# A 16-expert layer: the weights of experts 6 to 15 loaded as 32 KB rows into five buffers in place of 16 KB rows into ten

## The chip, the core and the metric

The kernel runs on one core of a Trainium2 chip. The metric is the device time of one execution in microseconds (us). The core has four compute engines with a queue each (TensorE, here PE; VectorE, DVE; ScalarE, ACT; GpSimd, POOL), a queue that only issues transfers (SyncE, SP), and 16 DMA engines that move data between the main memory (HBM) and the on-chip memory (SBUF, 128 partitions).

## The reference, cut to what matters

One layer on 512 tokens of width 1024, all in float32: a mixer (attention, convolution, gated linear attention), then a mixture of 16 experts. Each expert picks its 64 tokens, and its three weight matrices are read once.

```
x    = layer_norm(alpha * x + merged @ w_out) * ln_mix_g + ln_mix_b
aff  = softmax(x @ router_w);  gate, idx = top_k(aff.T, 64)      # per expert
xs   = x[idx]                                                    # 16 x 64 x 1024
h    = silu(xs @ w_gate) * (xs @ w_up)                           # w_gate, w_up: 16 x 1024 x 2048
y    = (h @ w_down) * gate                                       # w_down: 16 x 2048 x 1024
out  = layer_norm(alpha * x + scatter_add(y, idx))
```

The three matrices of an expert have 8 MiB each; all experts together have 402.7 MB.

## The kernel before, in words

The mixer and the router take the first third of the time. Then the experts run one after the other, `e` from 0 to 15, and each in three passes, `kind` in "gud" (gate, up, down), of eight steps `k` each. A step multiplies with one 1 MiB slice of the weight: 8 KB in each of the 128 partitions. `ff_mm` (L1218, its matmul L1223) does a step of gate and up, `down` (L1226, its matmul L1232) one of down, and `last_down` (L1254, its matmul L1265) one of the last expert's down pass.

Weights arrive as "pairs" (L824): 2 MiB transfers, 16 KB contiguous in each partition, for two steps each; so a pass has four pairs and an expert twelve. `load_pairs` (L828) issues them on SP in the order of use, through `load` (L78, L79 in the profile). Each takes one of the ten 16 KB buffers of the pool `pairs` (L35, NPAIR at L17), and waits until PE has done the two steps that used that buffer. The ten are used in one fixed rotation, which is not their order in memory: counted by address, the compiled program takes the buffers 6, 2, 8, 1, 0, 4, 3, 7, 9, 5 again and again, and the ten pairs from the third gate pair of expert 5 to its last down pair lie in this order. The compiled program also gives every transfer one of eight completion counters in turn, and a transfer's issue waits until the transfer that had the same counter before has landed.

What a partition holds is set by `halves` (L820): partition p holds r consecutive rows of the weight, r = 2 for gate and up (two rows of 2048) and r = 4 for down (four rows of 1024). Since gate and up multiply with a slice whose partition p stands for row 256 c + 2 p + b, the gathered tokens must be put in the same order: `gather` (L1167, its matmul L1171) reads every second column of the tokens, and its ACT instruction scales by the matching columns of `pkt`. In the same way the hidden values are transposed for the down pass with a column step of 4 (L1414). Tokens are gathered for two experts at a time, one pair of experts ahead: those of experts 6 and 7 in expert 5.

The last expert (`LAST`, 15) differs: its down weight is loaded by column blocks (first 512 columns, then twice 256) in ten transfers of 1 MiB to 256 KB with 2 KB and 1 KB rows, so that the first columns can be finished while the last ones arrive. The work on an expert's output is put off: `combine` (L1208, matmuls L1213 and L1214) adds a pair of experts to the sum in the up pass of the next even expert, one token block before each of the steps 5, 6 and 7 and one behind, and in the gate pass of expert 15. `st_pair` makes the transposed selection that `combine` needs, at the beginning of these passes.

PE's order is the order of the program text. SP's queue holds nothing but transfers, in the order above.

Of the kernel before, what the change touches and what calls it, by code (L numbers as in the profile page):

```python
# [5 lines left out]
F32 = mybir.dt.float32  # L6
# [17 lines left out]
PK_BIAS, PK_NG, PK_CW, PK_SINK, PK_RW, PK_LN, PK_N = 0, 4, 8, 20, 28, 156, 188  # L24
PK_G1, PK_B1 = PK_LN, PK_LN + 8


@with_exitstack
def tile_hybrid_layer(ctx, tc, pk, w2p, xT, x, wlv, wa, wak, wmb, wout, eg, eu, ed, gb, out):
    nc = tc.nc  # L30
# [3 lines left out]
    cpool = ctx.enter_context(tc.tile_pool(name="consts", bufs=1))  # L34
    dpool = ctx.enter_context(tc.tile_pool(name="pairs", bufs=NPAIR))  # L35
    spool = ctx.enter_context(tc.tile_pool(name="slots", bufs=NSLOT))
# [32 lines left out]
    def P(name):  # L69
        return psum.tile([128, 512], F32, name=name, tag="ps")  # L70
# [714 lines left out]
    def xr_(tb):  # L785
        return xres[tb // 2][:, tb % 2, :]
# [37 lines left out]
    chunk = {}  # L824
    pairs = [(e, kind, j) for e in range(NE) for kind in "gud" for j in range(4) if e or kind != "d" or j < 2]
    npair = [0]

    def load_pairs(upto):  # L828
        for e, kind, j in pairs[npair[0]:upto]:
            t = chunk[e, kind, j] = D(f"e{e}{kind}{j}", [128, 4096])[0]  # L830
            if kind != "d" or e < NE - 1:
                load(t, halves(e, kind, j))
                continue

            n, c = (8, slice(0, 512)) if j < 2 else (16, slice(j * 256, (j + 1) * 256))
            t = chunk[e, kind, j] = t.rearrange("p (f d) -> p f d", f=n)
            src = ed[e].rearrange("(f p) d -> p f d", p=128)[:, j % 2 * 8 if j < 2 else 0:, c]
            cuts = (0, n // 2, n) if j < 3 else (0, 8, 12, 14, 16)
            for f0, f1 in zip(cuts, cuts[1:]):
                load(t[:, f0:f1], src[:, f0:f1])  # L840
        npair[0] = max(npair[0], upto)

# [5 lines left out]
    def part(e, kind, k):  # L848

        t = chunk[e, kind, k // 2]  # L850
        return t[k % 2] if isinstance(t, list) else t[:, k % 2 * 2048:k % 2 * 2048 + 2048]

    for u in range(24):
# [6 lines left out]
        if u == 23:  # L860
            wo_split(0, 0)
            wo_split(0, 1)
            load_wo(1, None)
            load_pairs(EARLY)
            load_x()
        if u == 0:
            accs = D("macc", Q, Q)
# [299 lines left out]
    def gather(i, d):  # L1167

        p = P("pxg")
        for tb in range(4):  # L1170
            PE.matmul(p[:, 0:128], xr_(tb)[:, every2(d)], Sg[:, tb].rearrange("p a b -> p (a b)"),  # L1171
                      start=tb == 0, stop=tb == 3)
        A.activation(XG[i % 2][:, d, :], p[:, 0:128], AF.Identity, scale=pkt[:, PK_G1 + d:PK_G1 + d + 1],  # L1173
                     bias=pkt[:, PK_B1 + d:PK_B1 + d + 1])

# [67 lines left out]

    LAST = NE - 1
    gb2 = xres[0]
# [8 lines left out]
    def last_down(k):  # L1254

        b = max(k // 2 - 1, 0)
        n, m = (4, 512) if b == 0 else (8, 256)
        f0 = k * 4 if b == 0 else k % 2 * 8
        w = chunk[LAST, "d", k // 2][:, k % 2 * n:k % 2 * n + n]
        if f0 == 0:  # L1260
            st["py"] = P("py")
        py = st["py"][:, 0:m]
        for i in range(n):
            f, g = f0 + i, i % 2
            PE.matmul(py[g * 64:(g + 1) * 64, :], hT[:, f % 8, f // 8 * 64:f // 8 * 64 + 64], w[:, i, :],  # L1265
                      start=f < 2, stop=f >= 14)
        if f0 == 0 and b:
            last_combine(b - 1)
        gl = gate[:, LAST:LAST + 1]
        if f0 + n == 16:  # L1270
            h, l = ylast(yh, b), ylast(yl, b)
# [58 lines left out]
    for e in range(NE):  # L1330
        for kind in "gud":
# [6 lines left out]
            for k in range(8):  # L1338
# [3 lines left out]
                elif e % 2 == 1 and e < LAST:  # L1342
# [6 lines left out]
                    if s == 23:  # L1349
                        gates(i)  # L1350
                if e == 0 and kind == "u" and k == 0:
                    load_pairs(len(pairs))
# [44 lines left out]
            elif kind == "u":  # L1397
# [12 lines left out]
                for t in range(0, 8, n):  # L1410
                    p = P("pht")
                    for i in range(n):
                        c0, step = (t * 128 + i, 4) if e < LAST else ((t + i) * 128, 1)
                        PE.transpose(p[:, i * 128:(i + 1) * 128], hb[:, c0:c0 + 127 * step + 1:step], ident)  # L1414
# [72 lines left out]
def host_arrays(x, w_in, attn_sink, conv_w, gla_gate_w2, gla_gate_b, gla_norm_g, w_branch_attn, w_branch_conv,  # L1487
# [23 lines left out]
    for b in ("g", "c", "a"):  # L1511
        for j in range(8):
# [8 lines left out]
    rw = f(router_w)[0].reshape(4, 128, 2, 16).transpose(1, 0, 2, 3).reshape(128, 128)  # L1521
    col = lambda a: f(a)[0].reshape(8, 128).T
    col2 = lambda a: f(a)[0].reshape(4, 128, 2).transpose(1, 0, 2).reshape(128, 8)
    pk = np.concatenate([bias, ng, cw, rows(f(attn_sink)[0]), rw, col2(ln_mix_g), col2(ln_mix_b),
# [7 lines left out]
             eg=f(expert_w_gate)[0], eu=f(expert_w_up)[0], ed=f(expert_w_down)[0],  # L1532
             gb=np.concatenate([f(ln_ffn_g), f(ln_ffn_b)], 0))
    return {k: np.ascontiguousarray(v) for k, v in a.items()}
# [17 lines left out]
```

## Time and profile before

| | us |
|---|---|
| median of 3 runs (1434.36 to 1434.84) | 1434.37 |
| the profiled execution, its own time | 1432.91 |
| its span, first to last instruction | 1431.1 |
| PE busy in the span | 1356.2 |

The profiled execution spends 1.8 us outside its span. The page cuts the span into 40 slices of 35.8 us; a 9 in the DMA row means that the 16 DMA engines were busy at least 90% of the slice. TensorE's granted clock is at its full level nearly throughout.

### The profile page before, as it was taken

The numbers are of one execution on the slowest core, as the hardware profiler recorded it, in microseconds if no ns is written. First come the engines' busy times: TensorE is split into PE (matmuls) and PEld (weight loads), VectorE is DVE, ScalarE is ACT, GpSimd is POOL, SyncE is SP. The second block draws the span as 40 slices with busy tenths as digits, with TensorE's granted clock in tenths as the row PEclk, the third lists the DMA queues.
The fourth block names the chain that finished last, engine by engine and source line by source line (L and its number), as shares of the span: only waits on it lengthen the run. The fifth ranks groups of instructions, "written<-read, shape, count | busy, mean of one in ns | idle before, by whom it ended". The sixth has DMA issues, their size and how long they took to land.

```text
span 1431.1 us, 17334 instructions
## 1 busy us (share of the span) xinstructions
PE 1356.2 (95%) x7429; PEld 764.9 (53%) x7429; DVE 416.8 (29%) x875; ACT 291.7 (20%) x554; POOL 30.1 (2%) x57
## 2 busy tenths in 40 slices
PE   9999999999999899999999999988989898898997
PEld 8777777888888753443453443333333342343333
DVE  5593975323445513112012012002011010100314
ACT  4744544222233210110110110110000110011011
POOL 0010000000000010000000000000000000000002
PEclk9999999999999999999999999999999999999999
DMA  6120122223239789999999999999999999999995
GB/s 232 46 89 31 64 76 69 88 94 104 89 125 403 297 333 404 429 428 426 430 426 429 427 428 427 427 427 429 427 428 427 429 428 427 429 427 428 426 413 193
DMA packets 45456, 449.32 MB, mean 314 GB/s; under 512 B 4314, under 2 KB 8538, under 8 KB 19524
## 3 DMA queue, kind: packets, MB, share of 16 engines
q1 hardware_dynamic: 44804, 447.01, 75.6%
q8 instruction: 58, 0.95, 0.3%
q10 hardware_dynamic: 576, 1.21, 0.2%
q14 instruction: 18, 0.15, 0.0%
HBM read 446.11 MB, written 2.10 MB: 313 GB/s over the span
## 4 chain that ended last, share of the span: by engine, by line
PE 57%; DMA 37%; DVE 3%; SPq 1%; ACT 1%; issue 0%; DVEq 0%; POOL 0%; ACTq 0%
PE pgt L1223 7%; PE py L1232 6%; PE pup L1223 6%; PE pa L274 3%; PE pm L874 3%; PE pm L876 3%; PE pm L875 3%; DMA e8d<-in_ed_dram 3%; DMA e12g<-in_eg_dram 3%; PE pa L276 3%; PE pa L275 3%; DMA e9u<-in_eu_dram 3%; DMA e13u<-in_eu_dram 3%; DMA e10d<-in_ed_dram 3%; DMA e14u<-in_eu_dram 3%; DMA e6d<-in_ed_dram 3%
## 5 line engine op out<-in xcount | busy, mean ns | idle before, releaser
L1216 DVE TENSOR_TENSOR acc<-acc,pcb 128x512 f32<-128x512 f32 x64 | 41.1, 683 | 216.9 <-PE pcb L1214 216.9
L1401 DVE TENSOR_TENSOR hbt<-pup,hbt 128x512 f32<-128x512 f32 (+1 forms) x34 | 22.3, 660 | 279.0 <-PE pup L1223 278.9
L1171 PEld LDWEIGHTS pxg<-Sg,xres 128*128 128x128 f32 x512 | 65.2, 196 | 51.5 <-issue 46.8
L274 PE MATMUL pa<-xh,wb 128*128 128x512 f32 x200 | 82.7, 414 | 0.0
L1171 PE MATMUL pxg<-Sg,xres 128*128 128x128 f32 x512 | 76.2, 292 | 6.5 <-DVE Sg L1154 6.5
L276 PE MATMUL pa<-xh,wb 128*128 128x512 f32 x200 | 78.3, 391 | 0.0
L275 PE MATMUL pa<-xl,wb 128*128 128x512 f32 x200 | 78.2, 391 | 0.0
L874 PE MATMUL pm<-xh,wm 128*128 128x512 f32 x192 | 74.8, 390 | 0.0
L875 PE MATMUL pm<-xl,wm 128*128 128x512 f32 x192 | 74.7, 389 | 0.0
L876 PE MATMUL pm<-xh,wm 128*128 128x512 f32 x192 | 74.7, 389 | 0.0
L1241 DVE SCALAR_TENSOR_TENSOR yl<-py,small,late 64x512 fp32r<-64x512 f32 x30 | 22.5, 750 | 140.9 <-ACT late L1240 140.9
L1240 ACT ACTIVATE late<-py,small 64x512 fp32r<-64x512 f32 x30 | 20.5, 682 | 194.4 <-PE py L1232 182.3
L1173 ACT ACTIVATE xgb<-pxg,pk 128x128 f32<-128x128 f32 x32 | 14.6, 458 | 155.8 <-PE pxg L1171 155.8
L1415 ACT COPY hbt<-pht 128x512 f32<-128x512 f32 (+1 forms) x18 | 9.8, 550 | 169.9 <-PE pht L1414 169.4
L1173 ACT ACTIVATE xga<-pxg,pk 128x128 f32<-128x128 f32 x32 | 14.6, 457 | 142.6 <-PE pxg L1171 142.6
L274 PEld LDWEIGHTS pa<-xh,wb 128*128 128x128 f32 x200 | 37.5, 188 | 11.2 <-issue 2.9
L234 DVE TENSOR_TENSOR wm<-wr,wm 128x1536 fp32r<-128x1536 f32 x24 | 42.1, 1752 | 4.1 <-ACT wm L231 4.1
L1388 ACT ACTIVATE hbt<-pgt 128x512 f32<-128x512 f32 x32 | 19.0, 597 | 117.1 <-PE pgt L1223 117.1
L276 PEld LDWEIGHTS pa<-xh,wb 128*128 128x128 f32 x200 | 37.6, 188 | 8.4
L275 PEld LDWEIGHTS pa<-xl,wb 128*128 128x128 f32 x200 | 37.6, 188 | 6.4
L874 PEld LDWEIGHTS pm<-xh,wm 128*128 128x128 f32 x192 | 36.0, 188 | 7.6 <-issue 0.2
L876 PEld LDWEIGHTS pm<-xh,wm 128*128 128x128 f32 x192 | 36.0, 188 | 7.6
(426 smaller groups left out, 2264.6 us busy)
## 6 DMA issues: line engine op xcount, KB each, us to landing
wr<-in_wmb_dram SPq DMA_DIRECT2D x24, 768.0 KB, 4.3
wr<-in_wa_dram SPq DMA_DIRECT2D x12, 1024.0 KB, 4.8
e0g<-in_eg_dram SPq DMA_DIRECT2D x4, 2048.0 KB, 14.8
e0u<-in_eu_dram SPq DMA_DIRECT2D x4, 2048.0 KB
e1g<-in_eg_dram SPq DMA_DIRECT2D x4, 2048.0 KB, 7.7
e1u<-in_eu_dram SPq DMA_DIRECT2D x4, 2048.0 KB, 15.6
e1d<-in_ed_dram SPq DMA_DIRECT2D x4, 2048.0 KB, 15.0
e2g<-in_eg_dram SPq DMA_DIRECT2D x4, 2048.0 KB, 12.1
```

The source lines that it names most:

```text
L234: sp2[u] = V.tensor_sub(l, raw2[u], f32(h))
L274: PE.matmul(p, w[:, 0, k, :], XH(k), start=k == 0, stop=False)
L275: PE.matmul(p, w[:, 0, k, :], XL(k), start=False, stop=False)
L276: PE.matmul(p, w[:, 1, k, :], XH(k), start=False, stop=k == 7)
L874: PE.matmul(p, h[:, k, :], XH(k), start=k == 0, stop=False)
L875: PE.matmul(p, h[:, k, :], XL(k), start=False, stop=False)
L876: PE.matmul(p, l[:, k, :], XH(k), start=False, stop=k == 7)
L1171: PE.matmul(p[:, 0:128], xr_(tb)[:, every2(d)], Sg[:, tb].rearrange("p a b -> p (a b)"), start=tb == 0, stop=tb == 3)
L1173: A.activation(XG[i % 2][:, d, :], p[:, 0:128], AF.Identity, scale=pkt[:, PK_G1 + d:PK_G1 + d + 1], bias=pkt[:, PK_B1 + d:PK_B1 + d + 1])
L1216: V.tensor_add(r, r, p)
L1223: PE.matmul(p[c][g * 64:(g + 1) * 64, :], l, w[:, g * 1024 + c * 512:g * 1024 + c * 512 + 512], start=k == 0, stop=k == 7)
L1232: PE.matmul(p[g * 64:(g + 1) * 64, :], hT[:, k % 4 * 2 + r, half * 64:(half + 1) * 64], w[:, r * 1024 + dh * 512:r * 1024 + dh * 512 + 512 ...
```

## The change

For experts 0 to 5 nothing is changed but where the pool `pairs` lies (`side="right"`, and it can be released). For experts 6 to 15 (`EQ = 6`) a pass has two loads of 4 MiB, 32 KB contiguous in each partition, for four steps each. Gate and up hold four consecutive rows of the weight in a partition ("by fours"), down eight ("by eights"). At the beginning of expert 6's part of the program the pool of ten is released and a pool `fours` of five 32 KB buffers is opened; with `reuse_waits="tile"` a new buffer waits only for the old ones whose place it takes. The up weight of expert 15 comes in halves of 16 KB rows as before, and the pieces of its down weight are what they were, two of the old buffers' worth to one new buffer.

The row order goes with it: for experts from 6 on `gather` reads every fourth column and takes its scales from 16 columns of `pkt` that one more small transfer, `pk4`, fills behind `load_x`; the transposes of the hidden values step by 8 (expert 15: by 1, as before).

```diff
+PK_G4 = 0
+EQ = 6
-    dpool = ctx.enter_context(tc.tile_pool(name="pairs", bufs=NPAIR))
+    dpool = tc.alloc_tile_pool(name="pairs", bufs=NPAIR, side="right")
...
-    pairs = [(e, kind, j) for e in range(NE) for kind in "gud" for j in range(4) if e or kind != "d" or j < 2]
+    LAST = NE - 1
+    pairs = [(e, kind, j) for e in range(EQ) for kind in "gud" for j in range(4) if e or kind != "d" or j < 2]
...
+    def load_fours():
+
+        dpool.release()
+        qpool = ctx.enter_context(tc.tile_pool(name="fours", bufs=NPAIR // 2, side="right", reuse_waits="tile"))
+        for e, kind, j in ((e, kind, j) for e in range(EQ, NE) for kind in "gud" for j in range(2)):
+            t = chunk[e, kind, j] = qpool.tile([128, 8192], F32, name=f"e{e}{kind}{j}", tag="q")
+            if e < LAST or kind != "d":
+                r, w = (8, ed) if kind == "d" else (4, eg if kind == "g" else eu)
+                v = w[e].rearrange("(j p r) f -> j p (r f)", p=128, r=r)[j]
+                n = 2 if e == LAST and kind == "u" else 1
+                for c in range(n):
+                    c = slice(c * 8192 // n, (c + 1) * 8192 // n)
+                    load(t[:, c], v[:, c])
                 continue
...
+            for i in (2 * j, 2 * j + 1):
+                n, c = (8, slice(0, 512)) if i < 2 else (16, slice(i * 256, (i + 1) * 256))
+                v = t[:, i % 2 * 4096:i % 2 * 4096 + 4096].rearrange("p (f d) -> p f d", f=n)
+                last[i] = v
...
+        if e >= EQ:
+            return chunk[e, kind, k // 4][:, k % 4 * 2048:k % 4 * 2048 + 2048]
...
             load_x()
+            load(pkt[:, PK_G4:PK_G4 + 16], pk4)
...
-            PE.matmul(p[:, 0:128], xr_(tb)[:, every2(d)], Sg[:, tb].rearrange("p a b -> p (a b)"),
+            PE.matmul(p[:, 0:128], xr_(tb)[:, every2(d) if 2 * i < EQ else slice(c, c + 509, 4)], Sg[:, tb].rearrange("p a b -> p (a b)"),
...
+                if e == EQ and kind == "g" and k == 0:
+                    load_fours()
...
-                        c0, step = (t * 128 + i, 4) if e < LAST else ((t + i) * 128, 1)
+                        c0, step = (t * 128 + i, 4) if e < EQ else (t + i, 8) if e < LAST else ((t + i) * 128, 1)
```

## Rows read from the trace of the kernel before

**Rows 1.** The page's slices, 40 to the span: PE and DMA busy tenths, GB/s.
```profile
PE   9999999999999899999999999988989898898997
...
DMA  6120122223239789999999999999999999999995
GB/s 232 46 89 31 64 76 69 88 94 104 89 125 403 297 333 404 429 428 426 430 426 429 427 428 427 427 427 429 427 428 427 429 428 427 429 427 428 426 413 193
```
**Rows 2.** The chain that ended last, in order of time: start, us, what it was.
```profile
791.83 3.46 PE pup L1223 x16
795.30 37.78 DMA e6g<-in_eg_dram
...
833.15 39.20 DMA e6d<-in_ed_dram
...
1188.41 39.09 DMA e12d<-in_ed_dram
...
1286.47 39.21 DMA e14u<-in_eu_dram
1325.68 0.04 issue
1325.73 1.94 PE pup L1223 x8
```
**Rows 3.** SP's own waits from 840 to 1300 us: in total, times, longest.
```profile
SPq L79 <- DMA e7u<-in_eu_dram: 18.1, 4, 4.6
```
**Rows 4.** Stretches: busy time (and count) of PE, PEld, DVE, ACT, POOL; PEclk, DMA share, GB/s.
```profile
840.00:940.00 100.00, 92.26 (x476) 37.11 (x473) 11.76 (x21) 9.65 (x18) 0.00 (x0) 1.00 1.01 427
818.41:1350.15 531.74, 481.25 (x2424) 191.60 (x2422) 69.03 (x138) 49.46 (x89) 0.83 (x3) 1.00 1.01 428
455.45:460.44 4.99, 4.99 (x24) 4.13 (x23) 1.41 (x3) 0.00 (x0) 0.00 (x0) 1.00 1.01 420
1389.00:1394.00 5.00, 5.00 (x26) 1.71 (x22) 1.13 (x4) 0.09 (x1) 0.00 (x0) 1.00 1.04 381
```
**Rows 5.** DMA issues, 1350 to 1410 us: count, KB each, median us to landing.
```profile
e15d<-in_ed_dram SPq DMA_DIRECT2D x7, 1024.0 KB, 35.9
```
**Rows 6.** PE in order of time in experts 14 and 15: start, us, what, idle before.
```profile
1325.73 1.94 PE L1223 MATMUL pup<-e14u,xgb 128*64 128x512 f32 x8 [1.24 <-DMA e14u<-in_eu_dram]
...
1347.46 8.80 PE L1232 MATMUL py<-e14d,hbt 128*64 128x512 f32 x40
1356.09 1.89 PE L1223 MATMUL pgt<-e15g,xgb 128*64 128x512 f32 x8
...
1366.24 1.94 PE L1223 MATMUL pgt<-e15g,xgb 128*64 128x512 f32 x8
...
1394.87 7.21 PE L1265 MATMUL py<-e15d,hbt 128*64 128x512 f32 x32
1402.90 1.95 PE L1265 MATMUL py<-e15d,hbt 128*64 128x256 f32 x16 [0.83 <-DMA e15d<-in_ed_dram]
...
1410.04 1.95 PE L1265 MATMUL py<-e15d,hbt 128*64 128x256 f32 x16 [1.14 <-DVE yl L1273]
...
1413.06 1.95 PE L1265 MATMUL py<-e15d,hbt 128*64 128x256 f32 x16
```
**Rows 7.** PE's waits from 1325.7 to 1402 us, all there are.
```profile
PE pup L1223 <- DMA e14u<-in_eu_dram: 1.2, 1, 1.2
PE pbc L1117 <- DVE xga L1113: 0.3, 2, 0.2
PE py L1232 <- ACT hbt L1415: 0.2, 1, 0.2
```
**Rows 8.** PE in order of time at the end of expert 5.
```profile
802.77 5.37 PE L1223 MATMUL pup<-e5u,xga 128*64 128x512 f32 x24
...
817.55 7.09 PE L1232 MATMUL py<-e5d,hbt 128*64 128x512 f32 x32
...
827.22 3.17 PE L1223 MATMUL pgt<-e6g,xgb 128*64 128x512 f32 x13
```
**Rows 9.** DMA issues, 500 to 530 us, while the queue ran dry.
```profile
e1g<-in_eg_dram SPq DMA_DIRECT2D x3, 2048.0 KB, 7.7
```
**Rows 10.** Weight loads of the gather (step 2) and of L1414's transposes: min/median/max ns.
```profile
L1171 PEld LDWEIGHTS pxg<-Sg,xres x512: 193/196/208, 507.8 to 1284.5; 128*128 128x128 f32 x171
...
L1414 PEld LDWEIGHTS pht<-ident,hbt x16: 138/172/212, 1337.4 to 1394.6; 128*128 128x128 f32 x16
```
**Rows 11.** PE at the first expert's first step, in order of time.
```profile
509.89 1.94 PE L1223 MATMUL pgt<-e0g,xga 128*64 128x512 f32 x8
```

More of the change, by code (lines that the diff above doesn't have):

```diff
@@ L25, with tile_hybrid_layer @@
 PK_G1, PK_B1 = PK_LN, PK_LN + 8
+PK_G4 = 0
+EQ = 6
 @with_exitstack
-def tile_hybrid_layer(ctx, tc, pk, w2p, xT, x, wlv, wa, wak, wmb, wout, eg, eu, ed, gb, out):
+def tile_hybrid_layer(ctx, tc, pk, w2p, xT, x, wlv, wa, wak, wmb, wout, eg, eu, ed, gb, pk4, out):
     nc = tc.nc
@@ L830, in load_pairs @@
             t = chunk[e, kind, j] = D(f"e{e}{kind}{j}", [128, 4096])[0]
-            if kind != "d" or e < NE - 1:
-                load(t, halves(e, kind, j))
-                continue
[L835 to L841, printed above, removed]
+            load(t, halves(e, kind, j))
+        npair[0] = max(npair[0], upto)
+    def load_fours():
[10 more added lines that the diff above has]
+                    load(t[:, c], v[:, c])
+                continue
+            for i in (2 * j, 2 * j + 1):
+                n, c = (8, slice(0, 512)) if i < 2 else (16, slice(i * 256, (i + 1) * 256))
+                v = t[:, i % 2 * 4096:i % 2 * 4096 + 4096].rearrange("p (f d) -> p f d", f=n)
+                last[i] = v
+                w = ed[e].rearrange("(f p) d -> p f d", p=128)[:, i % 2 * 8 if i < 2 else 0:, c]
+                cuts = (0, n // 2, n) if i < 3 else (0, 8, 12, 14, 16)
+                for f0, f1 in zip(cuts, cuts[1:]):
+                    load(v[:, f0:f1], w[:, f0:f1])
+    last = {}
     def load_halves(j, tiles):
@@ L1167, in gather @@
     def gather(i, d):
-        p = P("pxg")
+        p, g1 = P("pxg"), PK_G1 if 2 * i < EQ else PK_G4
+        c = d // 4 * 512 + d % 4
         for tb in range(4):
-            PE.matmul(p[:, 0:128], xr_(tb)[:, every2(d)], Sg[:, tb].rearrange("p a b -> p (a b)"),
+            PE.matmul(p[:, 0:128], xr_(tb)[:, every2(d) if 2 * i < EQ else slice(c, c + 509, 4)], Sg[:, tb].rearrange("p a b -> p (a b)"),
                       start=tb == 0, stop=tb == 3)
-        A.activation(XG[i % 2][:, d, :], p[:, 0:128], AF.Identity, scale=pkt[:, PK_G1 + d:PK_G1 + d + 1],
-                     bias=pkt[:, PK_B1 + d:PK_B1 + d + 1])
+        A.activation(XG[i % 2][:, d, :], p[:, 0:128], AF.Identity, scale=pkt[:, g1 + d:g1 + d + 1],
+                     bias=pkt[:, g1 + 8 + d:g1 + 9 + d])
     def st_pair():
@@ L1242, in y_out @@
                                    op0=OP.mult, op1=OP.subtract)
-    LAST = NE - 1
     gb2 = xres[0]
@@ L1258, in last_down @@
         f0 = k * 4 if b == 0 else k % 2 * 8
-        w = chunk[LAST, "d", k // 2][:, k % 2 * n:k % 2 * n + n]
+        w = last[k // 2][:, k % 2 * n:k % 2 * n + n]
         if f0 == 0:
@@ L1522, in host_arrays @@
     col = lambda a: f(a)[0].reshape(8, 128).T
+    col4 = lambda a: f(a)[0].reshape(2, 128, 4).transpose(1, 0, 2).reshape(128, 8)
     col2 = lambda a: f(a)[0].reshape(4, 128, 2).transpose(1, 0, 2).reshape(128, 8)
@@ L1532, in host_arrays @@
              eg=f(expert_w_gate)[0], eu=f(expert_w_up)[0], ed=f(expert_w_down)[0],
-             gb=np.concatenate([f(ln_ffn_g), f(ln_ffn_b)], 0))
+             gb=np.concatenate([f(ln_ffn_g), f(ln_ffn_b)], 0),
+             pk4=np.concatenate([col4(ln_mix_g), col4(ln_mix_b)], 1))
     return {k: np.ascontiguousarray(v) for k, v in a.items()}
```

## The prediction

> **What bounds the kernel now.** I read the slices first. From the 17th slice on (about 570 us) the DMA row stands at 9 and the rate at 426 to 430 GB/s up to the last slice but one; PE is at 9 too [rows 1]. So two things are nearly full, and the chain of waits must say which of them ends last and where. The chain shows three parts. Up to 795 us it runs through PE. From 795.30 us to 1325.68 us it is nearly all transfers, each piece 39.1 to 39.3 us long [rows 2]; SP's own waits show why one piece is so long: every issue waits about 4.5 us for an earlier transfer to land (18.1 us in 4 waits) [rows 3], so eight 2 MiB transfers are always under way, and 39.1 / 8 = 4.9 us is the time of one. In that part PE waits for data. From 1325.73 us on PE is again without a hole: from there to 1402 us it waits 1.2 us once, which is the wait that begins this part, and 0.3 and 0.2 us for DVE and ACT [rows 7]. Only at the very end do two small waits come back, 0.83 us at 1402.90 and 1.14 us at 1410.04 [rows 6]. The second names DVE's yl, but that yl belongs to the column block just finished, and the matmul at 1410.04 is the first to read the next block of the weight; I take it as a wait for a transfer.
>
> So the end is set by a relay: DMA until the third up pair of expert 14 lands at 1325.68, then PE's own work of 76 us, then 2 us of waits for the last pieces.
>
> **Part 1, what a larger row saves.** In the long stretch the 16 engines move 428 GB/s [rows 4], so a 16 KB packet takes one engine 16 x 16384 B / 428 GB/s = 612.5 ns. In a stretch that holds nothing but the first 1 MiB pieces of expert 15's down weight [rows 5], with 2 KB rows, the rate is 381 GB/s [rows 4], 86.0 ns each. 14336 B more cost 526.5 ns, so 16 KB of pure bytes are 601.7 ns and a packet has a fixed part of about 10.8 ns. The stretch with 8 KB rows, 420 GB/s [rows 4], is 312.1 ns each, and twice that less 612.5 is 11.6 ns, about the same. Both short stretches are 5 us long, in which the rate is good to some 2%; I take 10 ns. A 4 MiB load has 128 rows, 8 for each engine, and 8 fixed parts fewer than two 2 MiB loads: 8 x 10 ns = 0.08 us of 9.8 us, 0.8%. No row of 32 KB is in this trace. The bounds are 0 (if the hardware cuts such a row in two, or the fixed part goes with bytes) and 0.1 us (12.5 ns); a loss I exclude from the range, as the rate only rises from 2 over 8 to 16 KB. I take 0.08, since the two sizes on either side of eightfold show it.
>
> From expert 6 to the second up load of expert 14 there are 8 x 6 + 4 = 52 such loads: 52 x 0.08 = 4.2 us earlier. To the gate pass of expert 15 there are 56: 4.5 us, and the pieces of expert 15's down weight, the same as before, come 4.5 us earlier too.
>
> The Trainium skill speaks against this size. Its page "DMA: Bandwidth & Descriptors", section "Why small descriptors are slow (HBM only)", gives a packet a fixed cost of about 3 cycles, which at the 850 MHz of the same page is an estimate of 3.5 ns, a third of what the rows give; by that page the 52 loads would save 52 x 8 x 3.5 ns = 1.5 us.
>
> **Part 2, what a larger load costs.** A load is usable when all of it has landed. Where PE keeps waiting for data this costs nothing, because the next load is late anyway: the DMA engines stay busy as long as loads are queued, and when a load lands four more are queued behind it, 4 x 9.7 = 39 us, while PE is done with it in about 9 us (four steps at 1.9 us [rows 6] and what lies between them). The price shows at the one place where PE's last unbroken run begins. There the third up pair of expert 14 lands at 1325.68 and the fourth one transfer later, at 1325.68 + 4.9 = 1330.6. After the change step 4 needs both in one: 1330.6 - 4.2 = 1326.4. PE's first four steps of that pass are over by then, as they need data that landed 9.7 us before and take 7.4 us. So PE's run begins 0.7 us later than before, not 4.2 us earlier. This is the step on which the forecast hangs.
>
> From there every step is PE's. The following loads are not late for it: step 4 of expert 15's gate pass stands at 1366.24 before [rows 6] and would be at 1367.0; its data would land at 1330.6 + 8 x 4.9 - 4.5 = 1365.3. The margin is 1.7 us, and it hardly changes if part 1 saves nothing (1369.8 against 1371.1). The up weight of expert 15 still comes in four pieces. So PE comes to expert 15's down pass at 1394.87 + 0.7.
>
> At that point the earlier data is worth something: the two waits of 0.83 and 1.14 us go, since their pieces land 4.5 us earlier and PE is only 0.7 us later. What is late next is PE itself, with its steps and the evacuation of each block. Sum: +0.7 - 0.83 - 1.14 = -1.3 us.
>
> **Part 3, the row order.** Transposes with a step of 8 in place of 4: their weight loads take 138 ns at step 1 and up to 212 at step 4, those of the gather 196 at step 2 [rows 10]. Bounds for step 8: nothing, and once more the 74 ns from 1 to 4, on 8 transposes of expert 14 that lie in PE's last run, 0.6 us. The rise from 2 to 4 is 16 ns, so I take 0.1 us. The gather at step 4 costs 32 loads x 16 ns = 0.5 us for two experts, in experts 5 to 13, where PE waits for data afterwards; without that cover it would be 2.5 us over five pairs. The new transfer pk4 (8 KB in 64-byte rows, issued on SP behind load_x) goes past nothing but the down pieces of expert 0. I bound it by 0 and 0.5 us; the first expert step starts at 509.89 [rows 11], long after these loads, so nothing waits. The 56 issues that SP saves are free: SP only waits.
>
> **Part 4, the switch at expert 6.** The first 32 KB buffer takes the place of two old ones, and SP issues in order. By the addresses the lowest two (0 and 1) hold expert 5's third and second up pair, whose steps end at 804.6 (the first third of the run that starts at 802.77) [rows 8]. The queue then still holds expert 5's down pairs; the third pair of expert 6 lands at 795.30 + 37.78 = 833.1 before, so expert 5's last pair, three transfers earlier, lands at 818.4. Issued at 804.6 the new load leaves no hole: 0 us. The second buffer could at worst lie on expert 5's last two down pairs, done at 822.9 and 827.2 [rows 8], and the DMA queue is fed till 818.4 + 9.7 = 828.1. If the first buffer is another one, there is a hole (below).
>
> **The sum.** -1.3 + 0.1 = -1.2 us on the profiled 1432.91, 1431.7; on the median, 1.5 us above it, 1434.37 - 1.2 = 1433.2.
>
> **Rivals.** (a) *Full gain.* If PE's last run has give that I don't see, the end follows the DMA: 4.5 us earlier, 1429.9. Rows 7 speak against it: hardly a wait in 76 us. Chance 0.12.
>
> (b) *No faster rows.* Part 1 saves nothing; then PE's last run begins a whole transfer later: +4.9 - 1.97 + 0.1 = +3.0, 1437.4. The slower side, then, is the same relay without its payment. It turns slower from the point where the 52 loads save less than 4.9 - 1.97 + 0.1 = 3.0 us, 0.058 us each. For it: no 32 KB row in the trace. Against it: the fixed part seen at 2 and at 8 KB. Chance 0.16.
>
> (c) *A smaller fixed part.* With 3 to 4 ns for a packet, below what the short stretches show, 52 loads save about 1.5 us: +3.4 - 1.97 + 0.1 = +1.5, 1435.9. By the skill's page named above it would be this. Chance 0.06.
>
> (d) *A hole at the switch.* If the first new buffer lies on one of the last two down pairs, its issue waits until 822.9 or 827.2, and from a dry queue a load lands after 7.7 us [rows 9], not 4.9: 2.8 us of start. 822.9 + 2.8 - 818.4 = 7.3 us, or 11.6 us, of idle DMA, all of it passed on, since all that follows is data and then PE: 1433.2 + 7.3 = 1440.5, or 1444.8. The same if the new pool waits for the whole old one. Chance 0.12.
>
> **How the numbers follow.** Forecast 0.54, (a) 0.12, (b) 0.16, (c) 0.06, (d) 0.12. The time is the forecast's, 1433.2. The range goes from (a) to (b), 1429.8 to 1437.6, and leaves out (d). This kernel's measurement can tell some 0.2% (2.9 us) from no change: faster is below 1431.5, (a) and a little of the forecast, 0.14; slower is above 1437.2, (d) and the larger part of (b), 0.22; the rest, 0.64, is no difference.
>
> **What would show it.** Part 1: 431 to 432 GB/s from 840 to 1340 us in place of 427 to 428, with half the packets; (b) shows 428. Part 2: a PE wait for e14u before step 4 (about 2 us), no wait after it up to expert 15's down pass, and the waits at its first and third column block gone. A PE wait for data inside experts 14 or 15 would mean that the relay is another. Part 4: the first e6g issue at about 804 us and no slice of DMA below 9 near 820 us; a dip there is (d). Part 3: transposes in expert 14 longer by over 0.1 us.

## The result and the profile after

| us | before | after |
|---|---|---|
| median | 1434.51 (6 runs) | 1446.41 (6 runs) |
| the profiled execution | 1432.91 | 1444.87 |
| its span | 1431.1 | 1443.1 |

The ratio is 1.0084, 95% interval 1.0071 to 1.0097: slower by 12 us, where 1.2 us faster was forecast. The six executions lie in two groups of three, near 1444.9 and near 1447.9 us, with the median between them, so how far another kernel's median lies from it is known to some 1.5 us. The profiled execution is the fastest; against the profiled one of before it is +12.0 us. Four questions lead through the new profile: is the DMA queue faster, is it ever empty, when does PE's last run begin, and is everything ahead of expert 6 still where it was?

First the page's slices of the changed kernel, the DMA and GB/s rows and the count of packets.

```profile
DMA  6120122223239789999999989999999999999995
GB/s 230 45 89 30 63 74 70 88 88 106 91 125 362 299 336 408 421 426 427 427 425 428 429 369 423 436 430 426 435 430 428 432 433 430 432 427 433 430 406 169
DMA packets 37535, 449.31 MB, mean 311 GB/s; under 512 B 3562, under 2 KB 7786, under 8 KB 18772
```

Against [rows 1] the slices behind the switch lie about 430, not 428, but the 24th (830 to 866 us) fell to 8 and 369 GB/s. From 840 to 1340 us the DMA view of the changed kernel says:

```profile
DMA packets 7400, 215.38 MB, mean 431 GB/s; under 512 B 816, under 2 KB 816, under 8 KB 816
```

The switch in stretches (columns: busy time and count of PE, PEld, DVE, ACT, POOL; granted clock, DMA share, GB/s):

```profile
820.00:836.00 16.00, 16.00 (x76) 9.52 (x78) 1.36 (x2) 1.96 (x4) 0.00 (x0) 1.00 0.82 350
836.00:850.00 14.00, 13.51 (x92) 7.55 (x90) 2.56 (x7) 1.36 (x2) 0.00 (x0) 1.00 0.85 349
850.00:862.00 12.00, 10.30 (x58) 3.84 (x56) 0.00 (x0) 2.27 (x4) 0.00 (x0) 0.98 0.98 422
```

There 18% of 16 us, 15% of 14 us and 2% of 12 us are missing, 5.2 us of idle DMA. (Counted by landings it is 4.4 us, the figure of the expectations below: the second load of e6g lands 12.6 us behind the first and the next one 11.3 us later, where 9.7 us is the time of one.) The chain of the changed kernel says who made the engines wait (start, us, what):

```profile
684.19 1.14 PE pxg L1195 x8
...
814.55 5.30 PE pup L1247 x24
819.86 2.06 PE pxg L1195 x8
821.92 0.95 PE pht L1439 x8
822.87 1.85 PE pxg L1195 x8
824.72 5.30 PE py L1256 x24
830.02 2.06 PE pxg L1195 x8
832.08 5.33 PE py L1256 x24
837.41 0.02 issue
837.42 11.94 DMA e6g<-in_eg_dram
```

The second load of expert 6's gate weight was issued at 837.42, when PE had done the third down pair of expert 5, and landed 11.94 us later out of an empty queue. What stands between the passes is the gather (pxg): 2.06 us each. Its rows, in the tile's view of the changed kernel (min/median/max ns of weight load and matmul; 8 gathers in this window):

```profile
L1195 PEld LDWEIGHTS pxg<-Sg,xres x64: 307/329/330, 783.0 to 831.6; 128*128 128x128 f32 x64
L1195 PE MATMUL pxg<-Sg,xres x64: 381/397/500, 783.0 to 831.7; 128*128 128x128 f32 x64
```

At step 2 a weight load of the gather took 196 ns [rows 10]; at step 4 it takes 329. A gather has 8 of them (four matmuls in the text, two records each in the trace), and a step-2 gather in the same chain, at 684.19, takes 1.14 us: 0.92 us more each, eight in expert 5, 7.4 us.

Then the end of the changed kernel, PE in order of time with the idle time before:

```profile
1340.08 1.94 PE L1247 MATMUL pup<-e14u,xgb 128*64 128x512 f32 x8 [2.68 <-DMA e14u<-in_eu_dram]
1380.58 1.94 PE L1247 MATMUL pgt<-e15g,xgb 128*64 128x512 f32 x8
1409.21 8.81 PE L1288 MATMUL py<-e15d,hbt 128*64 128x512 f32 x48
1420.13 3.67 PE L1288 MATMUL py<-e15d,hbt 128*64 128x256 f32 x32
1424.88 1.95 PE L1288 MATMUL py<-e15d,hbt 128*64 128x256 f32 x16
```

PE's last run begins with a wait of 2.68 us before step 4 of expert 14's up pass, and from there to expert 15's down pass it takes 69.13 us, as before (1394.87 less 1325.73 in [rows 6] is 69.14). The two waits at the blocks of the down pass are gone. From the begin of that down pass to the end of the span it is 33.9 us, 36.2 before.

And the part that I had not looked at, the mixer. The tile of its largest group of matmuls, before:

```profile
L875 PE MATMUL pm<-xl,wm x192: 389/389/402, 243.4 to 435.9; 128*128 128x512 f32 x192
```

and after:

```profile
L898 PE MATMUL pm<-xl,wm x192: 392/397/400, 246.1 to 442.9; 128*128 128x512 f32 x192
```

It begins 2.7 us later and ends 7.0 us later, with no wait added: matmuls that nobody edited are slower. From the start of one to the start of the next they are 0.234 us apart, not 0.227 (the mean over all of them in the trace). The first transfer of expert 1 is issued at 521.97 us, 514.88 before, and everything behind is late by that.

So the 12.0 us, in terms of when PE's last run can begin. The second load of e14u lands at 1340.0; the pair that held its last rows landed at 1330.6 before (1325.68 of [rows 2] and one transfer of 4.9): 9.4 us later, of which the mixer is 7.1, the hole 5.2 and the faster rows about -3.5 (428 to 431 GB/s make 9.80 us for 4 MiB into 9.73, 52 times); 0.6 us I can't place (1.4 with the hole at 4.4). Then 4.9 us because the whole load must have landed, and -2.3 us in the last pass: 9.4 + 4.9 - 2.3 = 12.0.

### The profile page after: what moved, and what is told of

It reads as the page before. It is cut to its first block, busy times and chain, and to the rows that moved or that the text cites. A ratio compares the mean times of both kernels' runs of the same rounds, so it can differ in the third digit from the quotient of the medians.

```text
span 1443.1 us, 17207 instructions
## 1 busy us (share of the span) xinstructions
PE 1396.5 (97%) x7429; PEld 816.4 (57%) x7429; DVE 417.0 (29%) x875; ACT 291.8 (20%) x554; POOL 29.8 (2%) x57
## 4 chain that ended last, share of the span: by engine, by line
PE 81%; DMA 15%; DVE 3%; ACT 1%; issue 0%; POOL 0%; ACTq 0%; DVEq 0%
PE pgt L1247 13%; PE pup L1247 12%; PE py L1256 11%; PE pxg L1195 8%; PE pa L276 3%; PE pm L897 3%; PE pm L898 3%; PE pm L899 3%; DMA e7g<-in_eg_dram 3%; DMA e11g<-in_eg_dram 3%; PE pa L278 3%; PE pa L277 3%; DMA e13g<-in_eg_dram 3%; DMA e14u<-in_eu_dram 3%; DMA e8u<-in_eu_dram 2%; PE pb L174 2%
## 5 line engine op out<-in xcount | busy, mean ns | idle before, releaser
L1195 PEld LDWEIGHTS pxg<-Sg,xres 128*128 128x128 f32 x512 | 102.1, 278 | 52.1 <-issue 52.0
L1195 PE MATMUL pxg<-Sg,xres 128*128 128x128 f32 x512 | 113.2, 364 | 6.5 <-DVE Sg L1177 6.5
L899 PEld LDWEIGHTS pm<-xh,wm 128*128 128x128 f32 x192 | 36.2, 188 | 8.8
L898 PEld LDWEIGHTS pm<-xl,wm 128*128 128x128 f32 x192 | 36.2, 188 | 8.6
```

The source lines that it names most:

```text
L898: PE.matmul(p, h[:, k, :], XL(k), start=False, stop=False)
L899: PE.matmul(p, l[:, k, :], XH(k), start=False, stop=k == 7)
L1195: PE.matmul(p[:, 0:128], xr_(tb)[:, every2(d) if 2 * i < EQ else slice(c, c + 509, 4)], Sg[:, tb].rearrange("p a b -> p (a b)"), start=tb ...
```

## The experiments

The working theory was this account: four terms, of which the forecast had two. Each run takes one out.

**Where the mixer's time went.** Only the layout differs there: the change puts the pool of ten at the upper end of SBUF, and with it the slots (a pool of five 8 KB buffers) and the small tiles move down. A matmul pm reads its moving operand, the tokens xh and xl, out of the slots, and its weights wm, which a weight load brings in first, out of the pool of ten.

```diff
-    dpool = ctx.enter_context(tc.tile_pool(name="pairs", bufs=NPAIR))
+    dpool = ctx.enter_context(tc.tile_pool(name="pairs", bufs=NPAIR, side="right"))
```

> The kernel before, with one edit: the pool of ten lies at the upper end of SBUF, as in the changed kernel. Theory 'placement': in the changed kernel the mixer's matmuls that read weights out of this pool are about 2% slower (8 columns' worth of them at 0.234 us each in place of 0.227), and the first e1g transfer is issued at 522.0 us and not at 514.9. So this edit alone moves that issue to about 522 us, and as PE, then the transfers, then PE again set the end, the time goes from 1434.5 to about 1441.6 us. Rival 'something else in the changed program' (the new small transfer, another schedule of the mixer): the issue stays at 515 and the time at 1434.5.

Measured: 1443.16 us, ratio 1.0061 (1.0046 to 1.0076); pm at 0.234 us, the first e1g issue at 523.60. The layout alone does it, in the kernel before. But which property of it? The next two shift the pool by 32 bytes, in the kernel before (the edit shown) and in the changed one.

```diff
-    dpool = ctx.enter_context(tc.tile_pool(name="pairs", bufs=NPAIR))
+    padp = ctx.enter_context(tc.tile_pool(name="pad", bufs=1, side="right"))
+    padp.tile([128, 8], F32, name="padt", tag="padt")
+    dpool = ctx.enter_context(tc.tile_pool(name="pairs", bufs=NPAIR, side="right"))
...
-    pkt = C("pk", [128, PK_N])
+    pkt = C("pk", [128, PK_N + 2])
...
-    one = X("one", [128, 2])
+    one = pkt[:, PK_N:PK_N + 2]
...
```

> The kernel before with the pool at the upper end of SBUF, but 32 bytes lower than in e1_right: its first byte in a partition is then at 65472, a multiple of 64, in place of 65504, which is one of 32 only (in the kernel before it is 1664, a multiple of 64). To make room, the two columns of ones move into the tile of constants. Theory 'alignment': the mixer's loss is gone, first e1g issue at about 515 us, time 1434.5. Rival 'place': the upper addresses themselves cost it, issue at 522 and time 1441.6.

> The changed kernel, with the pool 32 bytes lower, as in e2_right64. Theory 'three costs' (alignment 7.1 us, hole at the switch 4.4 us, relay in expert 14 4.9 us, against 0.07 us saved on each 4 MiB load): 1446.4 - 7.1 = 1439.3 us; the hole between the landings of e5d3 and e6u0 stays, because all of expert 5 moves forward by as much. Rival 'place': no change, 1446.4. Rival 'the 7 us are hidden by the hole': if the 7 us only used up time in which transfers would have waited anyway, 1446 too, with the first e1g issue at 515.

Measured: 1441.27 (1.0029 to 1.0065) and 1446.38 us, pm at 0.233 in both. The theory of alignment to 64 bytes fell, and with it the expected gain in the changed kernel. The next theory was the place of the moving operand:

```diff
+    spool = ctx.enter_context(tc.tile_pool(name="slots", bufs=NSLOT))
     dpool = ctx.enter_context(tc.tile_pool(name="pairs", bufs=NPAIR))
-    spool = ctx.enter_context(tc.tile_pool(name="slots", bufs=NSLOT))
```

> The kernel before with one edit: the pool of 8 KB slots, which holds the mixer's tokens (xh, xl), is allocated ahead of the pool of ten, so it lies at 1664 to 42624 in a partition in place of 165504 to 206464; the pool of ten begins at 42624 and the mixer's small tiles stay where they were. Since e2_right64 left the mixer slow, the theory is now 'moving operand low': the matmuls whose moving operand is xh or xl (pm, pa) have 0.234 us each when these tiles lie low and 0.227 when they lie high, while pbr, with its moving operand in the pool of ten, hardly changes. Then this kernel has pm at 0.233 to 0.234, its first e1g issue near 522 us, and 1441 to 1443 us. Rival 'pool of ten high' or 'small tiles low': pm stays at 0.227, 1434.5.

```diff
-    dpool = tc.alloc_tile_pool(name="pairs", bufs=NPAIR, side="right")
-    spool = ctx.enter_context(tc.tile_pool(name="slots", bufs=NSLOT))
+    dpool = tc.alloc_tile_pool(name="pairs", bufs=NPAIR)
+    padp = ctx.enter_context(tc.tile_pool(name="pad", bufs=1, side="right"))
+    padp.tile([128, 8], F32, name="padt", tag="padt")
+    spool = ctx.enter_context(tc.tile_pool(name="slots", bufs=NSLOT, side="right"))
...
-    mix = tc.alloc_tile_pool(name="mix", bufs=1)
+    mix = tc.alloc_tile_pool(name="mix", bufs=1, side="right")
...
```

> The changed kernel with the two sides exchanged: the pool of ten, and after it the five, keep the addresses that the ten have in the kernel before (1664 to 165504), and all else (slots, the mixer's tiles, the experts' tiles) goes to the other side, the slots at 188352 to 229312 (the two columns of ones move into the tile of constants for alignment). Theory 'moving operand low': pm back to 0.227 us, the first e1g issue at about 515, 1446.4 - 7.1 = 1439.3 us, with the hole at the switch as it was (e6g's second load lands 12.6 us after the first, the next one 11.3). Rival 'the pool can't be released without a cost in the mixer': 1446.4.

Measured: 1434.13 us (0.9986 to 1.0005) with the slots low, and 1442.96 us with the sides exchanged, pm at 0.2268 and 0.2296. That theory fell twice: low slots are fast, and high slots over a pool at its old addresses are slow. What the fast layouts had in common was a distance between the two pools that is a multiple of 512 bytes.

```diff
+    spool = ctx.enter_context(tc.tile_pool(name="slots", bufs=NSLOT))
+    kpool = ctx.enter_context(tc.tile_pool(name="pkc", bufs=1))
     dpool = ctx.enter_context(tc.tile_pool(name="pairs", bufs=NPAIR))
-    spool = ctx.enter_context(tc.tile_pool(name="slots", bufs=NSLOT))
...
-    pkt = C("pk", [128, PK_N])
+    pkt = kpool.tile([128, PK_N], F32, name="pk")
```

> The kernel before, with the slots ahead of the pool of ten as in e5_slots_low, and with the tile of 768 bytes that holds the small constants between the two. Against e5_slots_low the pool of ten and the mixer's small tiles keep their addresses to the byte; only the slots lie 768 bytes lower. The slots moved by 132 KB without any effect in e5_slots_low, so absolute addresses don't matter. Theory 'relative address': a pm matmul reads its moving operand (xh, xl in the slots) while the weights of the next one are read from the pool of ten, and the two reads disturb each other unless the pools lie a multiple of 512 bytes apart: 163840 and 40960 in the two fast kernels, 63840 (352 over) and 63808 (320 over) in the slow ones. Here it is 41728, 256 over: pm's matmuls at 0.230 to 0.235 us in place of 0.227, first e1g issue 3 to 8 us later than 515, 1437 to 1443 us. Rival 'something that only the upper end brings': pm at 0.227, 1434.5.

```diff
+    spool = ctx.enter_context(tc.tile_pool(name="slots", bufs=NSLOT))
-    dpool = tc.alloc_tile_pool(name="pairs", bufs=NPAIR, side="right")
+    dpool = tc.alloc_tile_pool(name="pairs", bufs=NPAIR)
-    spool = ctx.enter_context(tc.tile_pool(name="slots", bufs=NSLOT))
-    mix = tc.alloc_tile_pool(name="mix", bufs=1)
+    mix = tc.alloc_tile_pool(name="mix", bufs=1, side="right")
...
```

> The changed kernel with the layout turned round so that slots and pools stay a multiple of 512 bytes apart: slots first, then the pool of ten (and the five after it) at 42624, and the mixer's and the experts' small tiles on the other side. Theory 'relative address': pm's matmuls back at 0.227 us, first e1g issue at about 515, 1446.4 - 7.1 = 1439.3 us with the hole at the switch as it was. Rival 'the release costs the mixer': 1446.4.

Measured: 1434.15 us (0.9994 to 1.0012), pm at 0.2268: a distance of 256 over a multiple of 512 is fast, so 512 was wrong, while 128 and 256 stay possible. The changed kernel with its slots a multiple of 512 away: 1440.56 us (1.0035 to 1.0066), pm at 0.2268, e1g at 514.91: the mixer's loss is gone, the theory's 7.1 us came to 5.9 in the medians. In its trace a part of the rest is seen at the start of PE's last run:

```profile
1333.55 3.28 PE L1247 MATMUL pup<-e14u,xgb 128*64 128x512 f32 x8 [2.74 <-DMA e14u<-in_eu_dram]
```

The step begins 6.5 us earlier than in the changed kernel, but takes 3.28 us in place of 1.94: the granted clock from 1333.0 to 1336.2 us is 0.50. The last section comes back to this. Two runs then separate each operand's own address from the distance, with the same 32 bytes in two places:

```diff
+    padp = ctx.enter_context(tc.tile_pool(name="pad", bufs=1))
+    padp.tile([128, 8], F32, name="padt", tag="padt")
+    spool = ctx.enter_context(tc.tile_pool(name="slots", bufs=NSLOT))
     dpool = ctx.enter_context(tc.tile_pool(name="pairs", bufs=NPAIR))
-    spool = ctx.enter_context(tc.tile_pool(name="slots", bufs=NSLOT))
...
```

> The kernel before with the slots ahead of the pool of ten as in e5_slots_low, and 32 bytes of padding ahead of both (the two columns of ones move into the tile of constants to make room): slots at 1696, pool of ten at 42656, both 32 over a multiple of 128, their distance as in e5_slots_low. Theory 'own alignment': a matmul operand that doesn't begin at a multiple of 128 bytes is read more slowly; pm's matmuls take 0.230 to 0.236 us, the first e1g issue comes 4 to 10 us later than 515, 1438 to 1444 us. Rival 'distance': as the two pools are 40960 bytes apart, a multiple of 128, pm stays at 0.227 and the time at 1434.2.

```diff
+    spool = ctx.enter_context(tc.tile_pool(name="slots", bufs=NSLOT))
+    padp = ctx.enter_context(tc.tile_pool(name="pad", bufs=1))
+    padp.tile([128, 8], F32, name="padt", tag="padt")
     dpool = ctx.enter_context(tc.tile_pool(name="pairs", bufs=NPAIR))
-    spool = ctx.enter_context(tc.tile_pool(name="slots", bufs=NSLOT))
...
```

> e13_off32 with the 32 bytes of padding between the slots and the pool of ten in place of ahead of both: the pool of ten and everything above it keep their addresses to the byte, the slots lie 32 bytes lower (1664), and the distance is 40992, 32 over a multiple of 128. Theory 'distance': pm's matmuls take 0.230 to 0.236 us in place of 0.227, the first e1g issue comes 4 to 8 us later than in e13_off32 (516.4), and the time is 1438 to 1443 us. Rival 'not the distance either' (the slow layouts have something else in common): pm at 0.227, 1434.4.

With 32 bytes ahead of both pools, 1434.42 us (0.9993 to 1.0011):

```profile
L877 PE MATMUL pm<-xl,wm x192: 389/389/402, 244.9 to 437.4; 128*128 128x512 f32 x192
```

With 32 bytes between them, 1440.55 us (1.0026 to 1.0059):

```profile
L877 PE MATMUL pm<-xl,wm x192: 395/396/397, 247.2 to 444.0; 128*128 128x512 f32 x192
```

The first takes 192.5 us from first to last start, as before, the second 196.8. All layouts side by side:

| layout | distance of pool of ten and slots, bytes | over a multiple of 128 | pm, us from start to start |
|---|---|---|---|
| before | 163840 | 0 | 0.2268 |
| e5_slots_low, e10_slots_left, e13_off32 | 40960 | 0 | 0.2268 |
| e9_rel256 | 41728 | 0 | 0.2268 |
| e17_apart32 | 40992 | 32 | 0.2334 |
| e2_right64, e3_after64 | 63808 | 64 | 0.2333 |
| e6_mirror | 186688 | 64 | 0.2296 |
| after, e1_right | 63840 | 96 | 0.2341 |

In all eleven kernels of this table pm is fast where the distance is a multiple of 128 bytes and slow where it isn't, and e13_off32 and e17_apart32 together separate this from either operand's own address. The matmuls pbr, whose operands both lie in the pool of ten, are a control: 0.227 us before, 0.2275 after, at most 0.229 in the other slow layouts but one. That one is e6_mirror: at the same 64 bytes over, its pm loses less than in e2_right64, and its pbr are at 0.231, though their operands lie as far apart as before. So something acts there that these runs don't separate. Whether the period is 128 or 256 bytes, and what in the chip makes it so, stays open too.

**Where the hole comes from.** Two runs close it in two ways: faster gathers, or another order of the five places.

```diff
-            PE.matmul(p[:, 0:128], xr_(tb)[:, every2(d) if 2 * i < EQ else slice(c, c + 509, 4)], Sg[:, tb].rearrange("p a b -> p (a b)"),
+            PE.matmul(p[:, 0:128], xr_(tb)[:, every2(d)], Sg[:, tb].rearrange("p a b -> p (a b)"),
```

> The changed kernel, but the gather for experts from 6 on reads every second column, as before, so these experts get their features in another order than their weights have. Theory: the step of 4 makes one gather of a pair of experts 0.92 us longer, eight of them 7.4 us, all on PE in expert 5, which PE bounds; at step 2 expert 5's second up pair is done about 4.6 us and its third down pair about 7 us earlier, e6g's second load is issued near 830 us and not at 837.4, before e6g's first has landed (836.8), and the hole of 4.4 us is gone: 1446.4 - 4.4 = 1442.0 us. Rival 'order of the places': the hole comes from the order in which the new buffers take the old places, whatever the gathers last: 1446.4. Rival 'gathers on the path': the whole 7.4 us go, 1439.0.

```diff
-        qpool = ctx.enter_context(tc.tile_pool(name="fours", bufs=NPAIR // 2, side="right", reuse_waits="tile"))
+        qpool = ctx.enter_context(tc.tile_pool(name="fours", bufs=1, side="right", reuse_waits="tile"))
+        use = (0, 1, 3, 4, 2)
+        five = [qpool.tile([128, 8192], F32, name=f"q{i}", tag=f"q{i}") for i in range(5)]
+        five = [five[i] for i in use]
+        turn = (use[i % 5] for i in range(200))
...
```

> The changed kernel with the five places taken in the order 0, 1, 3, 4, 2 in place of 0, 4, 3, 2, 1, counted by address: e6g's second load then takes the place of expert 5's fourth gate pair and first down pair, and the place of the last down pair e5d3 is taken last. The slow gathers stay. Theory: a new load needs a place about every 9.7 us, and in this order the places come free in time (first down pair about 829 us, second 833, third 837, fourth 842, against landings at 836.8, 846.5, 856.2): no hole, 1446.4 - 4.4 = 1442.0. Rival 'the gathers alone make the hole' (PE is too late whatever the order): 1446.4.

Measured: 1442.83 us (1.0035 to 1.0071) and 1441.30 us (1.0032 to 1.0064), 3.6 and 5.1 us less than the changed kernel; 4.4 was expected of each. The first two stretches of e4_gather2, then all three of e7_order, to be held against those of the changed kernel above:

```profile
820.00:836.00 16.00, 14.88 (x98) 6.40 (x96) 0.88 (x2) 1.14 (x2) 0.00 (x0) 1.00 1.03 438
836.00:850.00 14.00, 11.46 (x54) 4.06 (x52) 1.68 (x6) 0.68 (x1) 0.00 (x0) 1.00 1.00 428
```


```profile
820.00:836.00 16.00, 16.00 (x76) 9.36 (x77) 1.12 (x2) 1.96 (x4) 0.00 (x0) 1.00 1.02 439
836.00:850.00 14.00, 14.00 (x94) 8.54 (x92) 2.56 (x7) 1.36 (x2) 0.00 (x0) 1.00 1.00 429
850.00:862.00 12.00, 12.00 (x66) 5.87 (x64) 0.00 (x0) 2.27 (x4) 0.00 (x0) 1.00 0.99 425
```

No share is missing any more. So the hole needs both: places in an unlucky order and a PE that is 7.4 us late. The rival that the gathers lie on the path by themselves wanted 1439.0 of e4_gather2. Its four executions, from 1439.40 to 1443.63, don't decide that well; e16_all3_gather2 below does: with the hole closed by the order of places, faster gathers give nothing.

**What the size of a load costs at the end.**

```diff
-                n = 2 if e == LAST and kind == "u" else 1
+                n = 2 if e >= LAST - 1 and kind == "u" else 1
```

> The changed kernel with the up weight of expert 14 in halves of 16 KB rows, as expert 15's is. Theory 'relay': PE's last unbroken run begins when the data for step 4 of that pass have landed; that is half a load earlier, 4.9 us, at 1335.2 and not at 1340.1. Of this about 1 us comes back as waits for the last pieces of expert 15's down weight: 1446.4 - 4.9 + 1 = 1442.5 us. Rival 'the end follows the transfers': the last run has no give of its own and the time goes by at most 1 us: 1445.4 to 1446.4.

Measured: 1447.95 us (1.0077 to 1.0109), no gain at all. PE in order of time:

```profile
1331.60 8.75 PE L1247 MATMUL pup<-e14u,xgb 128*64 128x512 f32 x40
1351.85 3.65 PE L1256 MATMUL py<-e14d,hbt 128*64 128x512 f32 x16 [0.47 <-DMA e14d<-in_ed_dram]
1371.30 3.04 PE L1247 MATMUL pgt<-e15g,xgb 128*64 128x512 f32 x8 [2.17 <-DMA e15g<-in_eg_dram]
```

The wait at e14u is gone, but new ones stand at e14d and e15g: the next whole loads are late for a PE that is now earlier. And behind the wait of 2.17 us the first step takes 3.04 us in place of 1.94; the granted clock from 1371.3 to 1374.8 us is 0.60. So the theory was right about the place and wrong about its extent. The same with halves for all that follows:

```diff
-                n = 2 if e == LAST and kind == "u" else 1
+                n = 2 if (e, kind) >= (LAST - 1, "u") or (e, kind) == (LAST - 1, "d") or e == LAST else 1
```

> The changed kernel with everything from the up weight of expert 14 on in halves of 16 KB rows. In e8_half14 PE began its last run 4.9 us earlier and then waited 2.2 us for e15g's first load and 0.5 us for e14d: the size of a load was paid again a few loads on. Theory 'relay over all the last loads': with halves there too, the run from step 4 of expert 14's up pass to expert 15's down pass has no wait again (69.1 us) and begins 4.9 us earlier; about 1.3 us come back at the last pieces, 1446.4 - 3.6 = 1442.8 us. Rival 'smaller rows cost the rate what they give': the halves land later and 1446.4 stays.

Measured: 1444.69 us (1.0062 to 1.0090), with no wait for data left from e14u on; 1.7 us less in the medians, 3.6 expected. The runs of either kernel spread over 2 to 3 us, so the size is uncertain here; the next block settles it.

**The forecast without the two costs that it lacked, and a kernel that beats both.** e12_all3 joins the edits of e10_slots_left, e7_order and e11_tail_halves; e14_two_mended is the change with layout and order mended only; e15_all3_16k takes the large rows out of e12_all3, and e16_all3_gather2 its slow gathers, with the edit of e4_gather2. The edit of e15_all3_16k against e12_all3 is the one line:

```diff
-                n = 2 if (e, kind) >= (LAST - 1, "u") or (e, kind) == (LAST - 1, "d") or e == LAST else 1
+                n = 2
```

> The three edits together in the changed kernel: the layout of e10_slots_left, the order of places of e7_order, the halves of e11_tail_halves. Theory: the costs are separate, so 1446.4 - 7.1 (mixer) - 5.1 (hole, as e7_order measured) - 3.6 (relay) = 1430.6 us, 0.27% less than the kernel before (1434.4). Rival 'one hides the other': over 1434.

> The changed kernel with the layout of e10_slots_left and the order of places of e7_order, nothing else: whole 4 MiB loads to the end. This is the change as the forecast had priced it. If its terms hold (52 loads 0.07 to 0.08 us faster, the last run of PE begun about 0.7 to 1.2 us later, about 2 us of waits gone), the time is 1433.2 us, as predicted, and 3 us above e12_all3. Rival: if the halves of e12_all3 gave more or less than 3.6 us, or the mended layout costs elsewhere, it lies outside 1432 to 1434.5.

> e12_all3 with every load from expert 6 on in halves of 16 KB rows, so that only the size of the rows and of the loads differs from it. Theory 'larger rows': a pair of halves takes 9.79 us in place of 9.72, and from expert 6 to the second up load of expert 14 that is 52 x 0.07 = 3.6 us: 1430.2 + 3.6 = 1433.8. Rival 'the rows give nothing at the end' (PE, not the transfers, sets it): 1430.2.

> e12_all3 with the gather of the later experts at a column step of 2 (their features then stand in another order than their weights). Theory: with the hole closed the slow gathers only make PE late in expert 5, by 7.4 us, and it catches up while it would wait for data: 1430.2, within 1 us. Rival 'the gathers also cost PE at the end or still hold up loads': 1426 to 1428.

| | measured, us | ratio to before | expected |
|---|---|---|---|
| e12_all3 | 1430.20 | 0.9979 (0.9970 to 0.9987) | 1430.6 |
| e14_two_mended | 1433.52 | 0.9994 (0.9985 to 1.0002) | 1433.2 |
| e15_all3_16k | 1434.43 | 1.0005 (0.9996 to 1.0014) | 1433.8 |
| e16_all3_gather2 | 1431.14 | 0.9981 (0.9971 to 0.9990) | 1430.2, within 1 |

All four fit. The rows of 32 KB are worth some 4 us at the end (e15 less e12: 4.2 in the medians, 3.7 by the ratios), the halves 2 to 3 us (e14 less e12: 3.3 and 2.2), and slow gathers nothing measurable once no load waits for them. By its interval e14_two_mended lies between 2.1 us under and 0.3 us over the kernel before: the forecast of -1.2 is in it, and so is no change, but not the rivals with +1.5, +3.0 or -4.5 us. PE in e14_two_mended, whose relay is that of the forecast:

```profile
1327.17 1.94 PE L1251 MATMUL pup<-e14u,xgb 128*64 128x512 f32 x8 [2.62 <-DMA e14u<-in_eu_dram]
1396.28 8.81 PE L1292 MATMUL py<-e15d,hbt 128*64 128x512 f32 x48
```

Against [rows 6] its last run begins 1.4 us later and is 69.1 us long. And e12_all3 is faster than the kernel before by 3.8 us in the medians (3.0 by the ratio), 0.2%; no run here is faster.

## Why the prediction was wrong

**The bound.** Right: PE, then transfers, then PE's last run. But the first sentence, "Up to 795 us it runs through PE", was read and then not used: whatever slows PE there is passed on whole. The forecast asked of `side="right"` only where the new buffers lie, not who else moves. That step was missing: the price of moving the other pools stood at nothing, without a reason. It was the largest term, 7.1 us in the first e1g issue, and e1_right with this edit alone takes 1443.16 us.

**Part 1, larger rows.** Right. 430 or 431 GB/s, half the packets, 0.07 us for a load against 0.08; that makes 3.5 us of 52 loads, and e15 less e12 gives 3.7 to 4.2, where 4.2 was forecast. Rival (b) is out. Rival (c) had 1.5 us for the same loads, worked out from the fixed cost that the Trainium skill's page "DMA: Bandwidth & Descriptors", section "Why small descriptors are slow (HBM only)", gives a packet; these runs show more than twice that.

**Part 2, the relay.** Right in the place, the wait (2.68 us), the length of the run and the vanished waits (-2.3 us against -1.97). In e14_two_mended the run begins 1.4 us later (0.7 forecast), and the time is 1433.52 against 1433.2; the two misses, +0.7 and -0.3, offset in part. "The following loads are not late for it" holds, since e15g's step 4 comes at 1380.58 without a wait; e8_half14 shows how thin that margin was.

**Part 3, the row order.** Here a term was mis-sized: "32 loads x 16 ns = 0.5 us" was 64 loads at 116 ns of time each, 7.4 us in expert 5. The 16 ns came from comparing transposes at step 4 (212 ns; over all experts their median is 211) with gathers at step 2 (196 ns): other instructions on other operands. No row of before had a gather at step 4, and the bound for it should have been as wide as that says. The transposes at step 8, priced at 0.1 us, cost nothing: eight in expert 14 take 1.06 us, 1.12 before. The Trainium skill's page "SBUF — State Buffer", section "Specifications (TRN2)", says that a line of 16 bytes must be hit at least twice for full bandwidth. Float32 at step 2 hits a line twice, at step 4 and 8 once: by that rule the jump lies between 2 and 4 and none follows. The trace agrees for the gathers (196, 329 ns) and for the last part (transposes no slower at 8 than at 4). It doesn't settle the whole: the transposes before, at step 4 too, load in 211 ns, near the gather's 196 at step 2, so the step alone doesn't set the price, and what else does is not shown.

The other half, "where PE waits for data afterwards", holds from expert 6 on (e16_all3_gather2), but expert 5 is ahead of the point where PE begins to wait.

**Part 4, the switch.** The first new load was issued at 816.46: 804.6 as forecast, 7.1 for the mixer and 4.6 for five slow gathers. The second took the place of the third down pair, one of the two that the text names as the worst; it said "done at 822.9" and a queue "fed till 828.1", a margin of 5.2 us. Both ends moved by the mixer, but PE by the gathers as well: 822.9 + 7.1 + 7.4 = 837.4, and at 837.42 it was issued. So the 0 that the forecast took had a cover, but the cover was checked without part 3's price. The sign named for rival (d), a dip of DMA at the switch, came; but (d) put the hole at the first buffer, and that its 7.3 us are near the 5.2 seen is chance.

## What to carry to other kernels

When a change moves pools, compare the distance of every pair of operands that a matmul reads, and look at stretches that the change doesn't touch: a loss with no new wait, in each instruction alike, is a sign of layout. Before a weight load takes a new stride, look for the trace's own row at that stride and count by the trace's records, then put the price into every margin that was found without it. Larger transfers give at the rate and take at the last hand-over to compute: keep them large while the compute engine waits anyway, and split all of the last ones, not one.

## What the runs showed of the hardware

- A float32 matmul of 128 x 512 whose moving operand and weights lie a multiple of 128 bytes apart in a partition takes 0.227 us from start to start in this mixer, and 0.230 to 0.234 us at 32, 64 or 96 bytes over. Own addresses 32 over make no difference (e13_off32). One layout, e6_mirror, has matmuls at 0.231 us without a change of distance.
- The gather's weight load of 128 x 128 float32 takes 196 ns with a column step of 2 and 329 ns with a step of 4; that of the transposes takes 211 ns with a step of 4 and at most 198 ns with a step of 8 in expert 14.
- With larger loads PE waits for data less often and longer: from 840 to 1420 us the changed kernel has nine such waits of over 1 us, 1.7 to 2.7 us long, the kernel before 34, all but one under 1.5 us. Behind three of the nine, and within 1 us, the granted clock fell for a short while to its lower level (1.2 GHz); in the trace of before it didn't fall between 510 and 1420 us. Two of the three stretches, the clock in the last column but two:

```profile
987.70:991.30 3.60, 3.60 (x10) 1.41 (x6) 0.19 (x1) 0.00 (x0) 0.00 (x0) 0.53 0.99 428
1134.40:1138.00 3.60, 3.60 (x9) 0.83 (x9) 1.66 (x5) 0.17 (x1) 0.00 (x0) 0.53 0.99 428
```

Ahead of the first PE had waited 2.63 us for e8u, ahead of the second 2.01 us for e11g. The six other waits, 2.68 us for e14u among them, were not followed by a fall, and the old loads are not quite free of one (e5_slots_low has one, at 1185.5 us). What sets the two kinds of wait apart, no run here shows. In the long stretch PE waits for data again later, so a fall there should cost little; that is argued, not measured. At the hand-over to PE's last run it costs: a step of eight matmuls took 3.0 to 3.3 us in place of 1.94 in the traces of e8_half14, e7_order and e10_slots_left, and the last run of e10_slots_left up to expert 15's down pass 70.5 us in place of 69.1.
